# Two-layer convolution and attention encoder on one core: wide gate products, one-product channel mean, reordered first loads, idle products in the last norm

## The chip, the cores and the metric

The kernel runs on one core of a Trainium2 chip. The metric is the time of the device in microseconds, from the start to the end of the program on that core; lower is better. Three runs of the kernel before gave 983.62, 984.91 and 985.09 us, the median is 984.91.

## What is computed

256 positions of width 2048 pass through two layers, all in fp32:

```python
for i in range(2):
    u = _rmsnorm(h, norm_g[i]) @ w_in[i]
    a_val, a_glu, a_z, q, k, v, b_z = split(u)
    ya = silu(_layernorm(conv31(a_val * sigmoid(a_glu)))) * silu(a_z)
    yb = window_attention(q, k, v) * silu(b_z)
    h = h + concatenate([ya, yb]) @ w_out[i]
    e = _rmsnorm(p[i] @ w_pe[i], pe_g[i])
    h = h + e * sigmoid(h @ w_pg[i])
return _rmsnorm(h, final_g)
```

`a_z`, the gate of the convolution group, is what the program calls `za`; `b_z`, the gate of the attention group, is `zb`. `ya` has 1024 channels in 8 tiles of 128, `yb` as well.

## The kernel before

All activations lie channel-first: 128 channels on the partitions, 256 positions along a row. A weight tile is a half of 1024 fp32 columns per partition, that is 8 blocks of 128 x 128. Halves are loaded two at a time, 1 MB, by SP (`load`, L154). Each half is then split into a high part, which ScalarE casts to fp32r (L163), and a low part, which VectorE gets by subtraction (L166). Activations are split in the same way (`hg`, `h`, `ya`, `yb`: index 0 is the high part and index 1 the low part). `mm3` (L387) multiplies a split weight with a split activation. For a 256-column output that is three products, high x high (L394), high x low (L395) and low x high (L396). Where the output is a whole bank of 2 x 256 columns, it is one 512-column product, the weight's high part with both parts of the activation side by side (L391), and one 256-column product (L392); the two sides of the bank must then be added, which `merge` (L398) does with a copy on ScalarE (L402) and an add on VectorE (L403). The output gate `g` uses the wide form (`wide`, L434); the input projection, the convolution gate `za` and the output projection use the narrow one (`pair`, L427).

The order of instructions on TensorE, VectorE and ScalarE is the order in which the program is written (`manual_schedule`, L130). `get` (L184) emits the splits four halves ahead of the products that use them, into five buffers. After each half, `pump` (L198) emits a few convolution taps (VectorE) and one step of every generator in `side`, where the attention heads and the channel norm wait. A bare `yield` in a generator puts what follows off to the next `pump`.

At the end of a layer's gate (L687 to L693) the program emits what is left of the convolutions (`finish`), casts the first pair of `yb` tiles, and applies the gate's Silu. The channel norm `lnorm` (L697) begins at once: the sum over channels is three products with a matrix of ones, of `ysum` (six tiles added up on GpSimd, L565) and of the last two tiles (L702). Its variance goes through `rstd_col` (L338), which multiplies the two halves of `vacc` with a column of ones. The output projection then takes 14 half steps with `yb` (L744), during which the norm finishes `ya`, and 14 with `ya`.

At the start the embedding products `e` (L490) use the first two weight tiles and `p` (L260), while x arrives in four quarters on ScalarE's DMA queue (L272) and ScalarE squares it for the first norm (L377, L380). At the end, `rstd_col` and `rstd_row` make the last norm's factor, three products keep TensorE occupied between them (L845), VectorE multiplies with the factor out of its PSUM bank, and GpSimd with a copy of it that ScalarE makes (L855).

Of the kernel before, what the change touches and what calls it, by code (L numbers as in the profile page):

```python
# [10 lines left out]
F32 = mybir.dt.float32  # L11
# [114 lines left out]
def trunk_kernel(ctx: ExitStack, tc: tile.TileContext, xT, pT, wst, par, gain, relb, sinkp, onehot, out):  # L126
# [136 lines left out]
    def load_half(c, x, n=1):  # L263

        if x == 0:
            raws[c] = wraw.tile([P, 2, HALF], F32, tag="raw", name=f"raw{c}")
        w = HALF // n
        for i in range(n):
            nc.sync.dma_start(raws[c][:, x, i * w:(i + 1) * w], wst[c, :, x * HALF + i * w:x * HALF + (i + 1) * w])

    def load_x(k):
        nc.scalar.dma_start(h[k // 8][:, k % 8:k % 8 + 4, :], xT[:, k:k + 4, :])  # L272

    h = halves(bigt("x"))
    pf = load_p(0)
    load_half(0, 0, 2)

    first = wk.tile([P, 2], F32, name="first", tag="rv")
    nc.scalar.activation(first, zeros[:, 0:2], AF.Square)
    for k in range(0, KT, 4):  # L280
        load_x(k)
    load_half(0, 1)
    load_half(1, 0)
    load_half(1, 1)
    gains = cst.tile([P, (DEPTH + 1) * KT], F32, name="gains")
    nc.sync.dma_start(gains, gain)
    load_half(2, 0)
# [50 lines left out]
    def rstd_col(parts, dim, name, between=None):  # L338

        c = bank(name + "c")  # L340
        for x, a in enumerate(parts):
            for b in range(2):
                nc.tensor.matmul(c[:, 0, b:b + 1], a[:, b * P:(b + 1) * P], ones[:, 0:1],
                                 start=(x == 0 and b == 0), stop=(x == len(parts) - 1), skip_group_check=True)
        v = wk.tile([P, 2], F32, name=name + "v", tag="rv")
        nc.vector.tensor_scalar(v, c[:, 0, 0:2], 1.0 / dim, EPS, ALU.mult, ALU.add)
        col = wk.tile([P, 2], F32, name=name + "col", tag="rcol")
        nc.gpsimd.tensor_tensor(col, v, mhalf, ALU.pow)
        if between:
            between()  # L350
        dg = wk.tile([P, 2, P], F32, name=name + "dg", tag="rdg", bufs=1)
        for b in range(2):
            nc.vector.tensor_scalar(dg[:, b, :], ident, col[:, b:b + 1], None, ALU.mult)
        return dg
# [42 lines left out]

    def merge(bs):  # L398

        t = wk.tile([P, 2, S], F32, name="hl", tag="ptt")[:, 0:len(bs), :]  # L400
        for x, b in enumerate(bs):
            nc.scalar.copy(t[:, x, :], b[:, 1, :])  # L402
            nc.vector.tensor_add(t[:, x, :], b[:, 0, :], t[:, x, :])  # L403
        return t
# [42 lines left out]
    for l in range(DEPTH):  # L447
# [239 lines left out]
        for t in range(0, NCT, 2):  # L687
            b = pair(hg, f"za{l}_{t}")
            if t == NCT - 2:
                finish(l)  # L690
                yb = bigt(f"yb{l}", F32R)
                nc.scalar.copy(yb[:, 0, 0:2, :], zb[:, 0:2, :])
            nc.scalar.activation(za[:, t:t + 2, :], b, AF.Silu)  # L693
# [3 lines left out]
        def lnorm(l=l, acc=acc, za=za, ya=ya, ysum=ysum, done=done):  # L697

            mb = bank("mean")
            parts = [ysum] + [acc[:, t, :] for t in done[-2:]]  # L700
            for x, a in enumerate(parts):
                nc.tensor.matmul(mb[:, 0, :], ones, a, start=(x == 0), stop=(x == len(parts) - 1))  # L702
# [11 lines left out]
            dg = rstd_col(halves_of(vacc), W_CONV, f"rv{l}")  # L714
# [126 lines left out]
    dg = rstd_col(hparts, D, "rf")  # L841

    wb = bank("warm2")
    for _ in range(3):
        nc.tensor.matmul(wb[:, 0, 0:P], ones, ident, start=True, stop=True)  # L845
    rb = rstd_row(dg, "rf", copy=False)
    rbs = wk.tile([P, S], F32, name="rfrb", tag="rb", bufs=1)

    for j in (0, 2, 12, 4, 6, 14, 8, 10):
        for x in [slice(0, 1), slice(1, 2)] if j == 0 else [slice(0, 2)]:  # L850
# [3 lines left out]
            if j == 0 and x.start == 0:  # L854
                nc.scalar.copy(rbs, rb)  # L855
# [78 lines left out]
```

## Time and profile before

| | |
|---|---|
| median of three runs | 984.91 us |
| the profiled execution | 983.99 us |
| its span, first to last instruction | 982.2 us |
| TensorE products, busy share of the span | 98% |
| VectorE | 79% |
| ScalarE | 57% |
| GpSimd | 9% |
| share of TensorE in the chain that ended last | 97% |
| HBM read | 177 MB, 185 GB/s over the span |

The profile comes from one execution. The busy share of an engine counts the time in which at least one of its instructions ran. Products are pipelined: a row's own duration is longer than the distance to the next row, and the distance is what the work costs. The chain that ended last is followed back from the last instruction, at each step to what released it.

### The profile page before, as it was taken

The numbers are of one execution on the slowest core, as the hardware profiler recorded it, in microseconds if no ns is written. First come the engines' busy times: TensorE is split into PE (matmuls) and PEld (weight loads), VectorE is DVE, ScalarE is ACT, GpSimd is POOL, SyncE is SP. The second block draws the span as 40 slices with busy tenths as digits, with TensorE's granted clock in tenths as the row PEclk, the third lists the DMA queues.
The fourth block names the chain that finished last, engine by engine and source line by source line (L and its number), as shares of the span: only waits on it lengthen the run. The fifth ranks groups of instructions, "written<-read, shape, count | busy, mean of one in ns | idle before, by whom it ended". The sixth has DMA issues, their size and how long they took to land.

```text
span 982.2 us, 18152 instructions
## 1 busy us (share of the span) xinstructions
PE 965.8 (98%) x7438; PEld 925.5 (94%) x7438; DVE 774.6 (79%) x1319; ACT 560.0 (57%) x862; POOL 86.6 (9%) x87
## 2 busy tenths in 40 slices
PE   8999999999999999999999999999999999999994
PEld 7999999999999999988899999999999999998884
DVE  4899989987787576687789998988887867667763
ACT  4655454777875554455566444568778545446551
POOL 0022001010000000011103200000100000100111
PEclk9999999999999999999999999999999999999997
DMA  7764636555544466446556555456454445654522
GB/s 287 254 238 171 213 131 215 189 178 181 166 153 177 149 238 225 172 172 230 198 184 237 175 203 181 172 188 204 146 168 165 172 143 200 217 191 162 197 104 86
DMA packets 29135, 182.49 MB, mean 186 GB/s; under 512 B 3723, under 2 KB 4284, under 8 KB 9212
## 3 DMA queue, kind: packets, MB, share of 16 engines
q1 hardware_dynamic: 24284, 165.17, 47.2%
q0 software_dynamic: 3472, 12.88, 4.4%
q10 hardware_dynamic: 1296, 3.28, 0.9%
q8 instruction: 58, 0.95, 0.4%
q14 instruction: 25, 0.20, 0.1%
HBM read 177.09 MB, written 4.23 MB: 185 GB/s over the span
## 4 chain that ended last, share of the span: by engine, by line
PE 97%; DVE 1%; DMA 1%; ACT 0%; POOL 0%; issue 0%; DVEq 0%; SPq 0%; ACTq 0%
PE g L391 12%; PE o L394 6%; PE o L395 6%; PE o L396 6%; PE ag L396 6%; PE ag L394 6%; PE ag L395 6%; PE g L392 6%; PE za L394 3%; PE zb L394 3%; PE q L394 3%; PE q L395 3%; PE zb L395 3%; PE za L395 3%; PE zb L396 3%; PE q L396 3%
## 5 line engine op out<-in xcount | busy, mean ns | idle before, releaser
L166 DVE TENSOR_TENSOR w<-raw,w 128x1024 fp32r<-128x1024 f32 x306 | 372.3, 1227 | 119.1 <-ACT w L163 116.1
L163 ACT CAST w<-raw 128x1024 fp32r<-128x1024 f32 x308 | 316.2, 1047 | 180.2 <-PE ag L396 45.1
L560 DVE SCALAR_TENSOR_TENSOR ac<-ac,pars 128x241 f32<-128x241 f32 (+11 forms) x480 | 217.9, 503 | 1.0
L391 PE MATMUL g<-h,w 128*128 128x512 f32 x496 | 175.3, 399 | 0.0
L396 PE MATMUL ag<-hg,w 128*128 128x256 f32 x512 | 145.2, 284 | 0.5 <-DVE w L166 0.5
L394 PE MATMUL ag<-hg,w 128*128 128x256 f32 x512 | 145.5, 284 | 0.0
L395 PE MATMUL ag<-hg,w 128*128 128x256 f32 x512 | 145.1, 283 | 0.1
L392 PE MATMUL g<-h,w 128*128 128x256 f32 x496 | 139.3, 281 | 0.0
L391 PEld LDWEIGHTS g<-h,w 128*128 128x128 f32 x496 | 93.2, 188 | 23.1
L394 PEld LDWEIGHTS ag<-hg,w 128*128 128x128 f32 x512 | 98.3, 192 | 0.9 <-ACT ac L553 0.9
L396 PEld LDWEIGHTS ag<-hg,w 128*128 128x128 f32 x512 | 98.3, 192 | 0.8 <-DVE w L166 0.7
L395 PEld LDWEIGHTS ag<-hg,w 128*128 128x128 f32 x512 | 98.3, 192 | 0.3 <-DVE hg L467 0.3
L392 PEld LDWEIGHTS g<-h,w 128*128 128x128 f32 x496 | 93.8, 189 | 0.0
L394 PE MATMUL za<-hg,w 128*128 128x256 f32 x256 | 73.7, 288 | 0.0
L394 PE MATMUL o<-yb,w 128*128 128x256 f32 x256 | 73.4, 287 | 0.0
L394 PE MATMUL q<-hg,w 128*128 128x256 f32 x256 | 73.3, 286 | 0.0
L394 PE MATMUL zb<-hg,w 128*128 128x256 f32 x256 | 73.2, 286 | 0.0
L395 PE MATMUL o<-yb,w 128*128 128x256 f32 x256 | 72.6, 284 | 0.0
L396 PE MATMUL o<-ya,w 128*128 128x256 f32 x256 | 72.5, 283 | 0.0
L394 PE MATMUL o<-ya,w 128*128 128x256 f32 x256 | 72.5, 283 | 0.0
L395 PE MATMUL o<-ya,w 128*128 128x256 f32 x256 | 72.5, 283 | 0.0
L396 PE MATMUL o<-yb,w 128*128 128x256 f32 x256 | 72.5, 283 | 0.0
(229 smaller groups left out, 2192.9 us busy)
## 6 DMA issues: line engine op xcount, KB each, us to landing
raw<-in_wst SPq DMA_DIRECT2D x153, 1024.0 KB, 4.9
bias<-fscr POOLq DMA_DIRECT2D x16, 384.0 KB, 3.8
raw<-in_wst SPq DMA_DIRECT2D x5, 512.0 KB, 9.8
x<-in_xT ACTq DMA_DIRECT2D x4, 512.0 KB, 7.1
hx<-in_xT POOLq DMA_DIRECT2D x8, 256.0 KB, 3.6
hscr<-e POOLq DMA_DIRECT2D x2, 1024.0 KB, 4.9
hx<-hscr POOLq DMA_DIRECT2D x8, 256.0 KB, 3.4
out_t<-og ACTq DMA_DIRECT2D x4, 256.0 KB, 3.0
```

What stands on the lines that cost most here:

```text
L163: nc.scalar.copy(hi, raw)
L166: nc.vector.tensor_sub(lo, raw, hi.bitcast(F32))
L391: nc.tensor.matmul(o, w[:, 0], x, start=start, stop=False, skip_group_check=True)
L392: nc.tensor.matmul(o[:, 1], w[:, 1], x[:, 0], start=False, stop=stop, skip_group_check=True)
L394: nc.tensor.matmul(o, w[:, 0], x[:, 0], start=start, stop=False, skip_group_check=True)
L395: nc.tensor.matmul(o, w[:, 0], x[:, 1], start=False, stop=False, skip_group_check=True)
L396: nc.tensor.matmul(o, w[:, 1], x[:, 0], start=False, stop=stop, skip_group_check=True)
L560: nc.vector.scalar_tensor_tensor(acc[:, t, lo_:hi_], a[:, t, lo_ + s:hi_ + s], w(k), acc[:, t, lo_:hi_], ALU.mult, ALU.add)
```

## The change

- `za` uses the wide form: each of the 8 tiles of a layer has a bank of its own and is merged by a copy and an add into its place in `za`; Silu then works on two merged tiles.
- The last two convolution tiles are added to `ysum` on VectorE, and the channel sum is one product. A `yield` ahead of it puts it one half step later.
- The variance's two halves are folded on VectorE ahead of `rstd_col`, which then has two small products instead of four.
- The first loads are dealt out anew over the queues of SP and ScalarE.
- In the last norm, five idle products stand between the small products of the two parts and four behind them; the factor is multiplied out twice, into a bank for VectorE and one for ScalarE's copy.

```diff
-    def load_half(c, x, n=1):
-
-        if x == 0:
+    def load_half(c, x, eng=nc.sync, n=1):
+
+        if c not in raws:
...
-    def load_x(k):
-        nc.scalar.dma_start(h[k // 8][:, k % 8:k % 8 + 4, :], xT[:, k:k + 4, :])
+    def load_x(k, eng=nc.sync):
+        eng.dma_start(h[k // 8][:, k % 8:k % 8 + 4, :], xT[:, k:k + 4, :])
 
     h = halves(bigt("x"))
+
+    load_half(0, 0, nc.scalar, 2)
     pf = load_p(0)
-    load_half(0, 0, 2)
-
-    first = wk.tile([P, 2], F32, name="first", tag="rv")
-    nc.scalar.activation(first, zeros[:, 0:2], AF.Square)
-    for k in range(0, KT, 4):
-        load_x(k)
     load_half(0, 1)
-    load_half(1, 0)
+    load_x(4, nc.scalar)
+    load_x(0)
+    load_half(1, 0, nc.scalar)
+    load_x(8)
+    load_x(12)
     load_half(1, 1)
+    load_half(2, 0)
     gains = cst.tile([P, (DEPTH + 1) * KT], F32, name="gains")
     nc.sync.dma_start(gains, gain)
-    load_half(2, 0)
     load_half(2, 1)
...
+    def idle(n):
+
+        wb = bank("idle")
+        for _ in range(n):
+            nc.tensor.matmul(wb[:, 0, 0:P], ones, ident, start=True, stop=True)
+
+    def rstd_col(parts, dim, name, between=None, idles=0):
 
         c = bank(name + "c")
         for x, a in enumerate(parts):
...
+            if x == 0 and idles:
+                idle(idles)
...
+    def merge1(t, b):
+
+        nc.scalar.copy(t, b[:, 1, :])
+        nc.vector.tensor_add(t, b[:, 0, :], t)
...
         for t in range(0, NCT, 2):
-            b = pair(hg, f"za{l}_{t}")
+            for x in range(2):
+                merge1(za[:, t + x, :], wide(hg, f"za{l}_{t + x}"))
             if t == NCT - 2:
                 finish(l)
+                for d in done[-2:]:
+                    nc.vector.tensor_add(ysum, ysum, acc[:, d, :])
                 yb = bigt(f"yb{l}", F32R)
                 nc.scalar.copy(yb[:, 0, 0:2, :], zb[:, 0:2, :])
-            nc.scalar.activation(za[:, t:t + 2, :], b, AF.Silu)
+            nc.scalar.activation(za[:, t:t + 2, :], za[:, t:t + 2, :], AF.Silu)
...
         def lnorm(l=l, acc=acc, za=za, ya=ya, ysum=ysum, done=done):
 
+            yield
             mb = bank("mean")
-            parts = [ysum] + [acc[:, t, :] for t in done[-2:]]
-            for x, a in enumerate(parts):
-                nc.tensor.matmul(mb[:, 0, :], ones, a, start=(x == 0), stop=(x == len(parts) - 1))
+            nc.tensor.matmul(mb[:, 0, :], ones, ysum, start=True, stop=True)
...
-            dg = rstd_col(halves_of(vacc), W_CONV, f"rv{l}")
+            dg = rstd_col([fold(vacc)], W_CONV, f"rv{l}")
...
-    dg = rstd_col(hparts, D, "rf")
-
-    wb = bank("warm2")
-    for _ in range(3):
-        nc.tensor.matmul(wb[:, 0, 0:P], ones, ident, start=True, stop=True)
+    dg = rstd_col(hparts, D, "rf", idles=5)
+    idle(4)
     rb = rstd_row(dg, "rf", copy=False)
+    rb2 = rstd_row(dg, "rf2", copy=False)
...
-                nc.scalar.copy(rbs, rb)
+                nc.scalar.copy(rbs, rb2)
```

Where it moves instructions, three places matter. The first is the end of the first layer's gate on ScalarE (`z` holds `za` and `zb`, `w` are split weights, `za_6` before is the bank of tiles 6 and 7). Before:

```order
L163 CAST w_3506<-raw_3356 128x1024
L163 CAST w_3534<-raw_3356 128x1024
L692 CAST yb_3561<-z_1613 128x512
L693 ACTIVATE z_1613<-za_6_3434 128x512
L736 CAST yb_3561<-z_1613 128x512 x3
L704 ACTIVATE mu<-mean 128x256
L163 CAST w_3587<-raw_3435 128x1024
```

And of the change:

```order
L163 CAST w_3410<-raw_3287 128x1024
L163 CAST w_3430<-raw_3287 128x1024
L408 COPY z_1611<-za_7_3407 128x256
L707 CAST yb_3453<-z_1611 128x512
L708 ACTIVATE z_1611<-z_1611 128x512
L750 CAST yb_3453<-z_1611 128x512 x3
L163 CAST w_3473<-raw_3352 128x1024
L718 ACTIVATE mu<-mean 128x256
```

The copy of the last gate tile now stands ahead of the first cast of `yb`, and `mu` comes behind one more weight cast.

The second place is the same end on VectorE, up to the variance (`ac` are the convolution tiles). Before:

```order
L166 TENSOR_TENSOR w_3534<-raw_3356,w_3534 128x1024
L737 TENSOR_TENSOR yb_3561<-z_1613,yb_3561 128x512 x4
L166 TENSOR_TENSOR w_3587<-raw_3435,w_3587 128x1024
L709 TENSOR_TENSOR ac_259<-ac_259,mu 128x512 x2
...
L381 TENSOR_TENSOR vacc<-vacc,sq 128x512
L166 TENSOR_TENSOR w_3658<-raw_3504,w_3658 128x1024
L166 TENSOR_TENSOR w_3685<-raw_3504,w_3685 128x1024
L166 TENSOR_TENSOR w_3714<-raw_3585,w_3714 128x1024
L346 TENSOR_SCALAR rv0v<-rv0c 128x2
```

And of the change:

```order
L409 TENSOR_TENSOR z_1611<-za_7_3407,z_1611 128x256
L705 TENSOR_TENSOR ysum_258<-ysum_258,ac_257 128x256 x2
L751 TENSOR_TENSOR yb_3453<-z_1611,yb_3453 128x512 x4
L166 TENSOR_TENSOR w_3473<-raw_3352,w_3473 128x1024
L166 TENSOR_TENSOR w_3504<-raw_3352,w_3504 128x1024
...
L389 TENSOR_TENSOR vacc<-vacc,sq 128x512
L166 TENSOR_TENSOR w_3575<-raw_3408,w_3575 128x1024
L166 TENSOR_TENSOR w_3604<-raw_3471,w_3604 128x1024
L166 TENSOR_TENSOR w_3631<-raw_3471,w_3631 128x1024
L376 TENSOR_TENSOR fold<-vacc 128x256
L354 TENSOR_SCALAR rv0v<-rv0c 128x2
```

Three adds now stand ahead of the low halves of `yb`, and the new fold stands behind three weight splits.

The third place is the start of SP's queue and of ScalarE's (`raw_85`, `raw_93` and `raw_98` are the first three weight tiles in the change). SP, with the change:

```order
L260 DMA p_88<-in_pT 128x512
L269 DMA raw_85<-in_wst 128x1024
L272 DMA x<-in_xT 128x1024 x3
L269 DMA raw_93<-in_wst 128x1024
L269 DMA raw_98<-in_wst 128x1024
```

ScalarE, with the change:

```order
L269 DMA raw_85<-in_wst 128x512 x2
L272 DMA x<-in_xT 128x1024
L269 DMA raw_93<-in_wst 128x1024
L385 ACT_TABLE_LOAD
L385 ACTIVATE hacc<-x 128x512
```

Before, ScalarE's queue held the four quarters of x and SP's `p` and all the weights; now three quarters of x stand on SP and the first half weight tile on ScalarE.

## Rows read from the trace of the kernel before

**Rows 1.** The page, busy time of an engine: us, share of the span, instructions.

```profile
PE 965.8 (98%) x7438; PEld 925.5 (94%) x7438; DVE 774.6 (79%) x1319; ACT 560.0 (57%) x862; POOL 86.6 (9%) x87
```

**Rows 2.** The windows, a stretch in the middle of the first layer's gate: length, then busy us (instructions) of TensorE, its weight loads, VectorE, ScalarE and GpSimd, the granted clock, the DMA share and GB/s.

```profile
250.00:300.00 50.00, 50.00 (x414) 47.35 (x413) 40.65 (x88) 35.12 (x68) 2.02 (x3) 1.00 0.52 172
```

**Rows 3.** The timeline of TensorE: start, duration, line, output and inputs. The first and the last of 24 gate products in a row, then the first and the 23rd 512-column product of the output gate.

```profile
249.84 0.28 PE L394 MATMUL za<-hg,w 128*128 128x256 f32 x1
...
252.60 0.28 PE L396 MATMUL za<-hg,w 128*128 128x256 f32 x1
...
399.99 0.40 PE L391 MATMUL g<-h,w 128*128 128x512 f32 x1
...
407.76 0.40 PE L391 MATMUL g<-h,w 128*128 128x512 f32 x1
```

**Rows 4.** The timeline at the end of the first layer's gate, TensorE, ScalarE and VectorE.

```profile
305.05 0.28 PE L396 MATMUL za<-hg,w 128*128 128x256 f32 x1
...
305.18 0.59 PE L702 MATMUL mean<-ysum,ones 128*128 128x256 f32 x2
...
306.59 0.28 PE L395 MATMUL o<-yb,w 128*128 128x256 f32 x1
...
303.44 0.62 ACT L692 CAST yb<-z 128x512 fp32r<-128x512 f32 x1
...
304.71 0.68 DVE L737 TENSOR_TENSOR yb<-z,yb 128x512 fp32r<-128x512 f32 x1
```

**Rows 5.** The timeline in the second layer's output gate: the product that follows a finished wide tile, the copy and the add of that tile, the VectorE operation behind it, and two adds of which the second needs the first.

```profile
961.04 0.28 PE L394 MATMUL g<-h,w 128*128 128x256 f32 x1
...
961.24 0.37 ACT L402 COPY hl<-g 128x256 f32<-128x256 f32 x1 [1.11 <-PE g L392]
...
961.64 0.42 DVE L403 TENSOR_TENSOR hl<-g,hl 128x256 f32<-128x256 f32 x1 [3.05 <-ACT hl L402]
...
961.99 0.41 DVE L797 TENSOR_TENSOR hs<-h 128x256 f32<-128x256 f32 x1
...
962.61 0.42 DVE L801 TENSOR_TENSOR e<-e,sg 128x256 f32<-128x256 f32 x1 [0.21 <-ACT sg L799]
...
963.07 0.43 DVE L802 TENSOR_TENSOR e<-e,hs 128x256 f32<-128x256 f32 x1
```

**Rows 6.** The timeline of the first channel norm's variance: the four small products (two instructions each) and the second projection product behind them, the row product, the three weight splits on VectorE, and the copy `mu` on ScalarE.

```profile
320.91 0.95 PE L343 MATMUL rv0c<-ones,vacc 128*128 128x1 f32 x8
...
321.92 0.28 PE L395 MATMUL o<-yb,w 128*128 128x256 f32 x1
...
324.68 0.59 PE L359 MATMUL rv0b<-rv0dg,ones 128*128 128x256 f32 x2
...
318.35 3.50 DVE L166 TENSOR_TENSOR w<-raw,w 128x1024 fp32r<-128x1024 f32 x3 [0.25 <-ACT w L163]
...
307.42 0.38 ACT L704 ACTIVATE mu<-mean 128x256 f32<-128x256 f32 x1
```

**Rows 7.** The timeline where the output projection passes from `yb` to `ya`: VectorE's last two low halves of `ya`, and TensorE's last product with `yb`.

```profile
345.86 1.52 DVE L730 TENSOR_TENSOR ya<-ac,ya 128x512 fp32r<-128x512 f32 x2
...
347.91 0.28 PE L395 MATMUL o<-yb,w 128*128 128x256 f32 x1
```

**Rows 8.** The start. First the DMA rate of the first 20 us in 40 equal slices, then two windows (columns as in Rows 2), then rows of the timeline: the first embedding products, the first norm product and a later wait on TensorE; the squares of x and copies on ScalarE; the fold on VectorE.

```profile
GB/s 0 0 0 53 119 397 373 406 299 176 201 205 266 336 344 406 397 414 426 451 393 410 426 418 434 401 410 434 387 390 395 401 393 399 392 426 260 227 475 410
...
8.00:9.00 1.00, 1.00 (x4) 0.77 (x3) 0.49 (x1) 0.48 (x1) 0.00 (x0) 0.50 1.01 406
...
11.00:12.00 1.00, 1.00 (x5) 0.87 (x4) 0.75 (x2) 0.64 (x2) 0.00 (x0) 0.82 1.04 422
...
7.07 10.56 PE L490 MATMUL e<-p,raw 128*128 128x256 f32 x40 [2.25 <-DMA raw<-in_wst]
...
17.46 0.50 PE L343 MATMUL rh0c<-ones,fold 128*128 128x1 f32 x4
...
31.98 0.39 PE L396 MATMUL ag<-hg,w 128*128 128x256 f32 x1 [0.51 <-DVE w L166]
...
7.33 0.63 ACT L377 ACTIVATE hacc<-x 128x512 f32<-128x512 f32 x1 [5.10 <-DMA raw<-in_wst]
...
12.48 0.58 ACT L514 COPY e<-e 128x512 f32<-128x512 f32 x1 [0.84 <-PE e L490]
...
14.21 0.59 ACT L514 COPY e<-e 128x512 f32<-128x512 f32 x1
...
14.69 0.63 ACT L380 ACTIVATE sq<-x 128x512 f32<-128x512 f32 x1
...
16.08 0.42 DVE L368 TENSOR_TENSOR fold<-hacc 128x256 f32<-128x256 f32 x1
```

**Rows 9.** The end: a window (columns as in Rows 2), the last row product on TensorE, VectorE's first and second output multiply, and ScalarE's copy between them.

```profile
971.00:971.50 0.50, 0.32 (x1) 0.35 (x2) 0.03 (x1) 0.00 (x0) 0.00 (x0) 0.50 0.00 0
...
971.18 1.19 PE L359 MATMUL rfb<-rfdg,ones 128*128 128x256 f32 x2 [0.88 <-DVE rfdg L353]
...
972.40 0.42 DVE L853 TENSOR_TENSOR og<-og,rfb 128x256 f32<-128x256 f32 x1 [1.38 <-PE rfb L359]
...
972.86 0.37 ACT L855 COPY rfrb<-rfb 128x256 f32<-128x256 f32 x1 [3.60 <-DVE og L853]
...
973.26 3.41 DVE L853 TENSOR_TENSOR og<-og,rfb 128x256 f32<-128x256 f32 x6 [0.44 <-ACT rfrb L855]
```

More of the change, by code (lines that the diff above doesn't have):

```diff
@@ L268, in load_half @@
         for i in range(n):
-            nc.sync.dma_start(raws[c][:, x, i * w:(i + 1) * w], wst[c, :, x * HALF + i * w:x * HALF + (i + 1) * w])
-    def load_x(k):
-        nc.scalar.dma_start(h[k // 8][:, k % 8:k % 8 + 4, :], xT[:, k:k + 4, :])
+            eng.dma_start(raws[c][:, x, i * w:(i + 1) * w], wst[c, :, x * HALF + i * w:x * HALF + (i + 1) * w])
+    def load_x(k, eng=nc.sync):
+        eng.dma_start(h[k // 8][:, k % 8:k % 8 + 4, :], xT[:, k:k + 4, :])
     h = halves(bigt("x"))
+    load_half(0, 0, nc.scalar, 2)
     pf = load_p(0)
-    load_half(0, 0, 2)
-    first = wk.tile([P, 2], F32, name="first", tag="rv")
-    nc.scalar.activation(first, zeros[:, 0:2], AF.Square)
-    for k in range(0, KT, 4):
-        load_x(k)
-    load_half(0, 1)
-    load_half(1, 0)
+    load_half(0, 1)
+    load_x(4, nc.scalar)
[3 more added lines that the diff above has]
+    load_x(12)
     load_half(1, 1)
+    load_half(2, 0)
     gains = cst.tile([P, (DEPTH + 1) * KT], F32, name="gains")
     nc.sync.dma_start(gains, gain)
-    load_half(2, 0)
     load_half(2, 1)
@@ L335, in load_bias @@
         return t
-    def rstd_col(parts, dim, name, between=None):
+    def idle(n):
[3 more added lines that the diff above has]
+    def rstd_col(parts, dim, name, between=None, idles=0):
         c = bank(name + "c")
@@ L401, in merge @@
         for x, b in enumerate(bs):
-            nc.scalar.copy(t[:, x, :], b[:, 1, :])
-            nc.vector.tensor_add(t[:, x, :], b[:, 0, :], t[:, x, :])
+            merge1(t[:, x, :], b)
         return t
```

## Prediction

> **What bounds the kernel now.** I read the page's busy shares first, then the windows by stage, then the start, the two turns from gate to output projection, and the end. TensorE is busy 98% of the span [rows 1], and in the middle of the convolution gate it is busy for all of 50 us at full clock while VectorE is busy for 40.65 and ScalarE for 35.12 [rows 2]. So time is gained in three ways only: fewer nanoseconds of TensorE per product, shorter TensorE waits at the two ends, or fewer products. And every new TensorE wait is paid in full.
>
> **Gate in 512-column products.** Per weight tile, three 256-column products become one of 512 and one of 256 columns. Old pace: 249.84 to 252.60 us holds 23 steps, 0.1200 each, 0.360 a triple. The output gate runs the new form already: 399.99 to 407.76 is 22 pairs, 0.3532 each [rows 3]. Both layers hold 2 x 8 x 16 = 256 triples, so 256 x 0.0068 = **-1.7 us**. The Trainium skill, page "TensorE: Matmul & The Clock Gate", section "Back-to-back issue gap", spaces warm products by columns / 2.4 GHz plus 2.5 ns; by that estimate triple and pair are 327.5 and 325.0 ns apart and the gain is 0.65 us, and the sum would be 1.1 us higher. The measured pace stands.
>
> The price is a copy on ScalarE and an add on VectorE for each of 16 tiles. Before the last tile of a layer they hide: split weights are made four steps of 2.9 us ahead, and the load rises by 0.37 and 0.42 us in 5.7, from the 70% and 81% of [rows 2].
>
> **The turn to the output projection: a new wait.** In the old program the cast of the first pair of `yb` stood ahead of the last gate instruction on ScalarE and ran at 303.44, its low half on VectorE at 304.71; TensorE's last gate product began at 305.05, so it was through by 305.17 and found both ready [rows 4]. Now the copy of tile 7 stands ahead of that cast, and it waits for TensorE's last gate product; on VectorE the tile-7 add and two `ysum` adds stand ahead of the low half. Call the end of the gate on TensorE T. The output gate shows the same step: TensorE goes on at 961.04, the copy starts at 961.24, the add at 961.64, the next VectorE operation 0.35 later [rows 5]. So: add at T + 0.60, first `ysum` add at T + 0.95, the second, which needs the first, about 0.46 later (the distance of 962.61 to 963.07, two dependent adds, [rows 5]), the first low half at T + 1.76, and with the 0.68 us of [rows 4] it ends at T + 2.45. The cast ends at T + 1.1, so one product runs and the second, which reads the low half, waits until T + 2.5 instead of T + 0.12: 2.4 us, and no other TensorE work stands there, since the change also puts the mean's product one step later. The following low halves are 0.61 apart and are there in time. Two layers: **+4.8 us**. Nothing covers it; neither engine can start before TensorE ends.
>
> **Channel norm.** With three mean products between, the second projection product began at 306.59; two steps of 0.12 after 305.05 would be 305.29 [rows 4]. So they took 1.30 us; one is left, 0.43. Two layers: **-1.7 us**. The variance's four small products took 320.91 to 321.92 less one step, 0.89 us; two are left, -0.45 [rows 6]. But the new fold stands on VectorE behind three weight splits. In the old order those ended at 321.85, 14.4 us after `mu` began at 307.42 [rows 6]. In the new one `mu` begins 3.45 us after the first projection step S (one step of 2.88, the mean, 0.15), the splits end at S + 17.9 and the fold at S + 18.2, while TensorE wants it after six steps and the mean, S + 17.7. It waits 0.5 to 0.6. Both layers: **+0.3 us**. What is late next is `ya`: its last low half ended at 347.38 and TensorE's last `yb` product began at 347.91 [rows 7], with the last pair of `ya` wanted six tiles of 0.36 later; the chain from the variance on moves by the same step as TensorE's, so I cost this at nothing, or 0.5 a layer if that cover is gone.
>
> **First loads.** The first weight piece now leads ScalarE's queue, so the embedding products can follow the warm-up ones instead of starting at 7.07. But x's first quarter now stands third on SP, behind `p` and half a weight tile, and lands together with the second, when `p`, the first weight tile and two quarters of x, 2.36 MB, have come: by the rates in [rows 8], added up, at 9.4 us, where the first square ran at 7.33. ScalarE then needs 1.73 us per group of one copy and two squares (12.48 to 14.21): copies at 10.5, 12.2 and 13.95, last square of the sum at 14.45, against 14.69. The fold, which ended at 16.50, ends near 16.3, and the first norm product can start at once; in the old run TensorE, slowed before, reached it only at 17.46 [rows 8]. What follows it hangs on it, so that distance moves whole: **-1.2 us**. Bounds: 0 if x comes later still, -2.4 if the 400 GB/s of 8 us on were there from 2.5 us, which puts 2.36 MB at 8.2.
>
> **The end.** The final row product took 1.19 us at granted clock 0.50 [rows 9]; the same product took 0.59 at full clock [rows 6] (its work 0.43). Idle products on both sides should hold the clock: -0.75. The second output multiply on VectorE waited for ScalarE's copy of the same bank, 972.40 to 973.26 [rows 9]; with a bank of its own it follows 0.35 later, another -0.45. The second row product costs only GpSimd's side, which still starts earlier. **-1.1 us**; if the clock falls all the same, -0.4.
>
> **TensorE's clock.** The old start shows a wait of 2.25 us ahead of the product at 7.07; 0.9 us after products resumed the granted clock fell to 0.50 and stayed there until 11.4 [rows 8], half of 3.4 us lost, 1.7. The new program has three such waits: 2.4 us at each turn, and about 2.5 us ahead of the first norm product, where the embedding products run out near 13.7. The 0.5 us wait at 31.98 was followed by no fall [rows 8]. Each could cost 0 to 1.7; I take one or two falls, partly beside other waits, **+1.8 us** (bounds 0 and 5.1).
>
> **Sum.** -1.7 + 4.8 - 1.7 + 0.3 - 1.2 - 1.1 + 1.8 = +1.2 us on the profiled execution's 983.99 (span 982.2), which is 0.9 under the median of the three runs, 984.91. So 985.2 for that execution, and **986.1 us** for a median. A measurement of this kernel tells about 0.2% from no change, 2.0 us: this is no change, on the slow side.
>
> **Rivals.**
> - *The clock falls at every new wait* (slower). Price 3 x 1.7 instead of 1.8: 989.4 us. For it: the only wait of that length in the trace did it. Against: the waits are broken by one product, and a fall at the start runs partly beside ScalarE's chain. It decides from the second full fall on. Chance 0.25.
> - *The first loads bring nothing.* The same bytes share the same engines: between 7 and 17 us the DMA runs near 400 GB/s already [rows 8], and x's first quarter comes later. Without the 1.2 us: 987.3. The Trainium skill, "DMA: Bandwidth & Descriptors", section "Issuing engines are not separate DMA queues", says that a second issuing engine saves only the issue time; the trace agrees as far as it goes, but here the order within the queues changes as well. Chance 0.08.
> - *No fall, and the early bytes come at the later rate* (faster). 986.1 - 1.8 - 1.2 = 983.1, and with waits shorter than reckoned below 982.9. For it: the rates of [rows 8] pass 400 GB/s once before 4 us. Chance 0.15.
> - *The idle products don't do what they say*: the clock falls before the last product, the second row product comes at half clock. The end gains 0.4: 986.8. Chance 0.07.
> - The forecast as summed: 0.45.
>
> **Numbers.** Faster 0.15; within 0.2% the forecast and the last rival, 0.52; slower the first two, 0.33. The range is 982.8 to 989.6: down to the third rival, up to the first.
>
> **What would show it.** Right: TensorE idle 2 to 2.5 us per layer ahead of the first two products `o<-yb`, put down to ScalarE's `yb` and VectorE's `yb`; gate pairs 0.353 apart; a first square near 9.4 and the first norm product near 16.3; `rfb` in about 0.45 us. Wrong: no idle time at the turns (then the result is 4 to 5 us faster), gate products waiting for banks or weights, or a first square before 8.

## The result, and the profile after

The changed kernel takes **987.21 us** (median of 18 executions, 984.60 to 988.71); the kernel before, run beside it, 984.14 us. The ratio is 1.0027, 95% interval 1.0020 to 1.0033: slower by a little more than the 0.2% that can be told. It lies inside the range of the prediction, above its 986.1 us and on the slow side, where "slower by over 0.2%" had 0.33; the outcome that the prediction held likeliest, within 0.2%, did not come. Two single executions among the experiments below, at 1891 and 2417 us, were in a slow state and are left out of every time given.

The profiled execution of the changed kernel is the quickest of the 18, 984.60 us with a span of 982.8. A fall below means that TensorE's granted clock goes from 1.00 to 0.50, that is from 2.4 to 1.2 GHz; in this execution there is none before the output multiplies. The others stand in steps above it: seven at 985.45 to 985.89, six at 987.09 to 987.88, four at 988.40 to 988.71, with a mean granted clock that goes down from 0.997 to 0.992. What the trace shows is therefore the change without falls of the clock; what a fall costs is read further down, from two traces that have two each.

**The page, and the gate's stretch** (compare [rows 1] and [rows 2]; columns as there).

```profile
PE 965.0 (98%) x7180; PEld 911.1 (93%) x7180; DVE 781.3 (79%) x1341; ACT 564.3 (57%) x877; POOL 86.7 (9%) x87
...
250.00:300.00 50.00, 50.00 (x306) 41.77 (x305) 41.50 (x92) 37.02 (x72) 2.02 (x3) 1.00 0.49 167
```

TensorE is as full as before, with 258 product instructions fewer in all. VectorE has 0.85 us more in these 50 us, ScalarE 1.9, and both have room left.

**The gate's pace** (timeline of TensorE; compare [rows 3]). The first and the eighth 512-column product of the gate:

```profile
249.18 0.40 PE L399 MATMUL za<-hg,w 128*128 128x512 f32 x1
...
251.65 0.40 PE L399 MATMUL za<-hg,w 128*128 128x512 f32 x1
```

Seven pairs in 2.47 us are 0.353 each, the pace that the output gate had.

**The turn to the output projection** (timeline of TensorE, then ScalarE, then VectorE; compare [rows 4]).

```profile
303.41 0.28 PE L400 MATMUL za<-hg,w 128*128 128x256 f32 x1
304.67 0.38 PE L402 MATMUL o<-yb,w 128*128 128x256 f32 x1 [0.98 <-ACT yb L707]
306.11 0.39 PE L403 MATMUL o<-yb,w 128*128 128x256 f32 x1 [1.05 <-DVE yb L751]
306.33 0.28 PE L404 MATMUL o<-yb,w 128*128 128x256 f32 x1
...
308.96 0.59 PE L716 MATMUL mean<-ysum,ones 128*128 128x256 f32 x2
...
303.72 0.37 ACT L408 COPY z<-za 128x256 f32<-128x256 f32 x1 [1.72 <-PE za L400]
303.99 0.62 ACT L707 CAST yb<-z 128x512 fp32r<-128x512 f32 x1
...
309.60 0.38 ACT L718 ACTIVATE mu<-mean 128x256 f32<-128x256 f32 x1 [1.77 <-PE mean L716]
...
303.10 1.22 DVE L166 TENSOR_TENSOR w<-raw,w 128x1024 fp32r<-128x1024 f32 x1
304.24 0.42 DVE L409 TENSOR_TENSOR z<-za,z 128x256 f32<-128x256 f32 x1
304.57 0.87 DVE L705 TENSOR_TENSOR ysum<-ysum,ac 128x256 f32<-128x256 f32 x2
305.37 0.68 DVE L751 TENSOR_TENSOR yb<-z,yb 128x512 fp32r<-128x512 f32 x1
```

The gate ends at T = 303.53, 0.12 after its last product begins. The first product with `yb` runs at T + 1.14, the second at T + 2.58. Between them stand exactly the instructions named: copy and cast on ScalarE; tile 7's add, the two `ysum` adds and the low half on VectorE. VectorE was still busy with a weight split when the copy was done, so tile 7's add began at T + 0.71. Layer 2 has the same waits, 0.98 and 1.05.

**The variance** (TensorE, then VectorE; compare [rows 6]).

```profile
324.63 0.58 PE L349 MATMUL rv0c<-ones,fold 128*128 128x1 f32 x4 [0.68 <-DVE fold L376]
...
320.65 3.50 DVE L166 TENSOR_TENSOR w<-raw,w 128x1024 fp32r<-128x1024 f32 x3 [0.25 <-ACT w L163]
324.07 0.42 DVE L376 TENSOR_TENSOR fold<-vacc 128x256 f32<-128x256 f32 x1
```

**The start** (TensorE, ScalarE, VectorE; compare [rows 8]).

```profile
16.80 0.50 PE L349 MATMUL rh0c<-ones,fold 128*128 128x1 f32 x4
...
9.69 0.63 ACT L385 ACTIVATE hacc<-x 128x512 f32<-128x512 f32 x1 [5.73 <-DMA x<-in_xT]
...
15.79 0.42 DVE L376 TENSOR_TENSOR fold<-hacc 128x256 f32<-128x256 f32 x1
```

**The end** (TensorE, VectorE, ScalarE; compare [rows 9]).

```profile
972.75 0.67 PE L367 MATMUL rfb<-rfdg,ones 128*128 128x256 f32 x2 [0.65 <-DVE rfdg L361]
...
973.45 3.74 DVE L865 TENSOR_TENSOR og<-og,rfb 128x256 f32<-128x256 f32 x7 [0.85 <-PE rfb L367]
...
973.88 0.37 ACT L867 COPY rfrb<-rf2b 128x256 f32<-128x256 f32 x1 [3.05 <-PE rf2b L367]
```

The row product takes 0.67 instead of 1.19, and VectorE multiplies seven times without a break.

Where TensorE stands in the two traces, in us, by the start of the product named:

| | before | changed | difference |
|---|---|---|---|
| first projection product | 24.27 | 23.62 | -0.65 |
| first gate product, layer 1 | 249.84 | 249.18 | -0.66 |
| last gate product, layer 1 | 305.05 | 303.41 | -1.64 |
| first product with `ya`, layer 1 | 348.15 | 348.61 | +0.46 |
| first gate product, layer 2 | 726.09 | 726.54 | +0.45 |
| last gate product, layer 2 | 781.30 | 780.77 | -0.53 |
| first product with `ya`, layer 2 | 824.40 | 825.97 | +1.57 |
| `rfb` | 971.18 | 972.75 | +1.57 |
| end of the span | 982.2 | 982.8 | +0.6 |

The gate gives 0.98 a layer, the turn with the norm takes 2.10 back, the start gives 0.65 and the end 0.97.

### The profile page after: what moved, and what is told of

Its sections match the earlier page's. It is cut to its first block, busy times and chain, and to the rows that moved or that the text cites. A ratio compares the mean times of both kernels' runs of the same rounds, so it can differ in the third digit from the quotient of the medians.

```text
span 982.8 us, 17671 instructions
## 1 busy us (share of the span) xinstructions
PE 965.0 (98%) x7180; PEld 911.1 (93%) x7180; DVE 781.3 (79%) x1341; ACT 564.3 (57%) x877; POOL 86.7 (9%) x87
## 4 chain that ended last, share of the span: by engine, by line
PE 87%; DVE 7%; ACT 3%; issue 1%; DMA 0%; POOL 0%; DVEq 0%; ACTq 0%
PE g L399 12%; PE ag L404 6%; PE ag L402 6%; PE ag L403 6%; PE g L400 6%; PE o L403 5%; PE o L404 5%; PE o L402 5%; PE zb L402 3%; PE q L402 3%; PE zb L403 3%; PE q L403 3%; PE zb L404 3%; PE q L404 3%; DVE w L166 3%; PE za L399 3%
## 5 line engine op out<-in xcount | busy, mean ns | idle before, releaser
L399 PE MATMUL za<-hg,w 128*128 128x512 f32 x256 | 92.2, 402 | 0.0
```

Of the source, the lines that this page charges most:

```text
L399: nc.tensor.matmul(o, w[:, 0], x, start=start, stop=False, skip_group_check=True)
```

## Experiments

My theory was the prediction's: the loss is TensorE's wait at the two turns, and in the other executions a fall of its clock there. The rivals: the spread comes from the new start; the wide tiles alone make the wait; something else is late next. Times are medians, with the lowest and the highest execution behind them.

**Order at the turn (e_turn).** A gate tile takes two half steps, one for each weight half; in tile 7 all of `yb` now goes between them, and GpSimd adds the last two convolution tiles to `ysum`:

```diff
-            if 2 <= len(done) <= NCT - 2:
+            if 2 <= len(done):
...
-                merge1(za[:, t + x, :], wide(hg, f"za{l}_{t + x}"))
+                b = bank(f"za{l}_{t + x}")
+                step(b, hg, True, False)
+                if t + x == NCT - 1:
...
+                    for i in range(0, 8, 2):
+                        hilo(yb[:, 0, i:i + 2, :], yb[:, 1, i:i + 2, :], zb[:, i:i + 2, :])
+                step(b, hg, False, True)
+                merge1(za[:, t + x, :], b)
...
-                for d in done[-2:]:
-                    nc.vector.tensor_add(ysum, ysum, acc[:, d, :])
```

> The change, but all four casts and low halves of yb are put between the two half steps of gate tile 7, and the last two convolution tiles are added to ysum on GpSimd; the rest is as changed. Theory A (the loss is TensorE's wait at the two turns, 0.98 + 1.05 us per layer in the profiled execution, and in other executions a fall of the clock at these waits): no wait at the turn, 2 x 2.0 = 4.1 us gone, and with it the 2.6 us by which the median of 18 runs, 987.21, stands above the execution without a fall, 984.6: about 980.6 us, single runs within some 1 us. Rival B (the spread of single runs comes from the start or from elsewhere): 987.2 - 4.1 = 983.1 us, and single runs still 4 us apart. Rival C (the wait is hidden by something else that is late next, such as ya): 985 to 987 us with a new wait ahead of the ya products.

985.06 us (983.12 to 987.56). The wait at the turn shrank as meant, but the theory's 980.6 us failed: rival C came true, at the variance instead of `ya`. Waits of TensorE in this trace (what it waited for: us in total, times, longest):

```profile
PE rv1c L349 <- DVE fold L376: 1.9, 1, 1.9
...
PE rv0c L349 <- DVE fold L376: 1.0, 1, 1.0
PE o L403 <- DVE yb L456: 1.0, 3, 0.4
...
PE mean L721 <- POOL ysum L577: 0.5, 1, 0.5
```

ScalarE's timeline of layer 2 shows why; the mean began at 783.75:

```profile
784.28 0.63 ACT L713 ACTIVATE z<-z 128x512 f32<-128x512 f32 x1 [3.70 <-DVE z L409]
784.81 1.03 ACT L163 CAST w<-raw 128x1024 fp32r<-128x1024 f32 x1
785.75 0.38 ACT L723 ACTIVATE mu<-mean 128x256 f32<-128x256 f32 x1
```

`mu` stands behind Silu, which waits for VectorE's add of tile 7, and behind a weight cast: 2.0 us after the mean, where the change has 0.64. Counted from the first gate product of layer 2, TensorE's second `yb` product had become 1.9 us earlier than in the change, `mu` only 0.1: the norm's chain kept its old time. After the 1.9 us wait the clock fell to 0.50, at 801.

**Idle products in the turn (e_idle).**

```diff
  ob = [bank(f"o{l}_{j}") for j in range(NB_FIRST // 2)]
+ idle(9)
```

> The change plus nine idle products between the last gate product and the first product of the output projection in each layer, some 2.4 us of TensorE work that nothing needs: the turn is as long, but TensorE is occupied in it. Theory A (the clock falls at the turns in other executions than the profiled one): 984.6 to 985.2 us, single runs within some 1.5 us. Rival B (falls or spread from elsewhere): 987.2 us, single runs 4 us apart as before.

984.90 us (984.10 to 986.47): 2.3 us less than the change, with work added. The turn is as long, the second `yb` product at T + 2.59, and the trace has no fall there; so what went is the clock's falls at the turns. Some spread is left. In the profiled execution TensorE waited 1.3 us for the first norm's fold and the clock fell at 18, which puts at least a part of it at the start.

**Narrow gate (e_narrow).**

```diff
- for x in range(2):
-     merge1(za[:, t + x, :], wide(hg, f"za{l}_{t + x}"))
+ b = pair(hg, f"za{l}_{t}")
...
- nc.scalar.activation(za[:, t:t + 2, :], za[:, t:t + 2, :], AF.Silu)
+ nc.scalar.activation(za[:, t:t + 2, :], b, AF.Silu)
```

> The change with the convolution gate narrow again (a bank of two tiles, three 256-column products, Silu out of the bank); ysum on VectorE, one mean product, loads and end as changed. The gate takes 1.7 us more. Theory A (add and ysum adds both stand in the way; without the add the two ysum adds and the low half still come 1.2 to 1.4 us after the gate's end, because VectorE is through with its weight splits only then): 984.6 + 1.7 - 2 x 0.7 = 984.9 us without falls, 985 to 987 as a median. Rival D (the copy and the add of the wide tile alone make the wait): 984.6 + 1.7 - 4.1 = 982.2 us, with a narrow spread.

983.88 us (983.47 to 985.24), between the two, and 3.3 us below the change:

```profile
PE o L403 <- DVE yb L750: 1.6, 2, 0.8
```

TensorE waits 0.8 us per layer, before the second product alone, because the `ysum` adds (303.75 to 304.55) still stand ahead of the low half. So the wide tile makes about 1.2 of the 2.0 us. With waits of 0.8 us the executions lie within 1.8 us, and the trace has no fall at either turn. The other four parts of the change together are worth nothing that can be told against the kernel before: ratio 1.0001 (0.9992 to 1.0009).

**Old first loads (e_loads).**

```diff
-    load_half(0, 0, nc.scalar, 2)
     pf = load_p(0)
+    load_half(0, 0, n=2)
...
+    for k in range(0, KT, 4):
+        load_x(k, nc.scalar)
     load_half(0, 1)
-    load_x(4, nc.scalar)
-    load_x(0)
-    load_half(1, 0, nc.scalar)
-    load_x(8)
-    load_x(12)
+    load_half(1, 0)
     load_half(1, 1)
-    load_half(2, 0)
...
```

> The change with the first loads in the old order on the old queues. Theory A: the first gate-side product comes 0.65 us later, as in the two traces (24.27 against 23.62), and the spread at the turns stays: 987.2 + 0.7 = 987.9 us. Rival B (the new start is what makes single runs differ by 4 us): a narrow spread, about 985.3 us. Rival E (the reordered loads bring nothing): 987.2 us.

986.61 us, which eight executions do not tell from the change's 987.21; theory A's 987.9 failed. The eight lie on three levels: 985.10 and 985.22; 986.53, 986.58 and 986.63; 988.21, 988.21 and 988.51. Steps of 1.4 and 1.7 us would fit none, one or two falls at the turns, but only the execution at 985.22 has a trace (it has none), and the one at 986.53 has a mean granted clock of 0.997, the same as that trace, in which 3.4 us at half clock, 0.0017 of the mean, do not fit. With 3.4 us of spread left, the new start is not what makes the change's 4.1. That it adds to it is seen across the traces: with the new loads the first projection product comes anywhere from 23.04 to 24.86 (the nine traces that start as the change does), with the old from 24.02 to 24.32 (four).

**Reordered version (e_best).** Against the change:

```diff
-            if 2 <= len(done) <= NCT - 2:
+            if 2 <= len(done) <= NCT - 1:
...
+                step(b, hg, True, False)
+                if t + x == NCT - 1:
...
+                    for i in range(0, 8, 2):
+                        hilo(yb[:, 0, i:i + 2, :], yb[:, 1, i:i + 2, :], zb[:, i:i + 2, :])
+                        if i == 2:
+                            nc.vector.tensor_add(ysum, ysum, acc[:, done[-1], :])
+                step(b, hg, False, True)
...
             nc.scalar.mul(mu, mb[:, 0, :], 1.0 / W_CONV)
+            nc.scalar.activation(za[:, NCT - 2:NCT, :], za[:, NCT - 2:NCT, :], AF.Silu)
...
+            fv = fold(vacc)
             yield from wait(LY[0])
-            dg = rstd_col([fold(vacc)], W_CONV, f"rv{l}")
+            dg = rstd_col([fv], W_CONV, f"rv{l}")
```

> The change with three orders of work altered and nothing else: the casts and low halves of yb stand between the two half steps of gate tile 7, with the add of the last convolution tile to ysum between them (the tile before it is added on GpSimd); the last Silu of za stands behind the cast mu; the fold of vacc stands ahead of the three weight splits. Theory F (in the first such run the gain was eaten by VectorE's and ScalarE's queue: mu came 2.0 us after the mean instead of 0.64, because Silu and a weight cast stood ahead of it, and the fold then kept TensorE 1.0 and 1.9 us): both waits go, 2 x (2.03 - 0.5) + 2 x 0.7 = 4.5 us less than the execution without falls, 980.1 us; median 980 to 981.5 us, the rest being the start. Rival G (the two layer ends are bound by VectorE's total work from the gate to ya, so that a wait comes back ahead of the last ya products or of the variance): 983 to 985 us.

**979.63 us** (978.64 to 980.08, five executions), ratio to before 0.9949 (0.9936 to 0.9961): 4.4 us below the kernel before. Theory F holds. Of the turn, 0.4 us per layer are left, of the variance nothing; the one fall in its trace is at the start.

```profile
PE rh0c L349 <- DVE fold L376: 1.3, 1, 1.3
...
PE o L403 <- DVE yb L456: 0.8, 2, 0.4
```

**Old mean (e_mean).**

```diff
-                for d in done[-2:]:
-                    nc.vector.tensor_add(ysum, ysum, acc[:, d, :])
...
-            yield
             mb = bank("mean")
-            nc.tensor.matmul(mb[:, 0, :], ones, ysum, start=True, stop=True)
+            parts = [ysum] + [acc[:, t, :] for t in done[-2:]]
+            for x, a in enumerate(parts):
+                nc.tensor.matmul(mb[:, 0, :], ones, a, start=(x == 0), stop=(x == len(parts) - 1))
```

> The change with the old mean: three products at once behind the gate, ysum of six tiles alone, no half step's delay; wide gate, fold, loads and end as changed. Theory A (at the turn the copy, the add and the ysum adds all stand ahead of yb, and the mean's products no longer cover it): the three products cover 1.3 us, the low half of yb ends 0.87 us earlier, 0.3 us of 2.03 remain; minus 2 x 1.7, plus 2 x 0.87 for the products: 984.6 - 1.7 = 982.9 us without falls, and as the waits are short, no falls: median 983 to 983.8 us. Rival D (the wide tile's copy and add alone make the wait): 984.6 + 1.7 = 986.3 us or more.

985.07 us (983.91 to 986.38), five of the eleven executions at 983.91 to 984.49; theory A's 983 to 983.8 was missed.

```profile
PE rv0c L349 <- DVE fold L376: 1.3, 1, 1.3
...
PE o L403 <- DVE yb L750: 1.1, 4, 0.3
```

The turn behaved as meant (two waits of up to 0.3 per layer, no falls there in the trace), so rival D is out; but the fold now keeps TensorE 1.3 us per layer instead of 0.7. With the mean one half step earlier, the variance's products come earlier too, and the three splits ahead of the fold do not.

**Fold ahead of the splits (e_fold).**
```diff
+ fv = fold(vacc)
  yield from wait(LY[0])
- dg = rstd_col([fold(vacc)], W_CONV, f"rv{l}")
+ dg = rstd_col([fv], W_CONV, f"rv{l}")
```

> The change with the fold of vacc ahead of the three weight splits on VectorE. Theory: TensorE's 0.7 us wait ahead of the variance goes in both layers, 1.4 us less: 983.2 us without falls, median 985.5 to 986 us, the turns being as they are. Rival G (ya is late next: its last low half ended 0.05 us before TensorE wanted it): the gain is lost again ahead of the last ya products, 987 us.

985.64 us (984.65 to 986.79). The wait ahead of the variance is gone, and none came ahead of `ya`: as expected. The profiled execution happens to have the clock's fall at both turns. Windows of layer 1 (columns as in [rows 2], the granted clock is the third number from the end):

```profile
304.50:305.00 0.50, 0.00 (x0) 0.00 (x0) 0.50 (x2) 0.50 (x2) 0.00 (x0) 1.00 1.00 164
305.00:305.50 0.50, 0.00 (x0) 0.00 (x0) 0.50 (x2) 0.50 (x2) 0.00 (x0) 1.00 0.44 82
305.50:306.00 0.50, 0.47 (x4) 0.48 (x5) 0.50 (x2) 0.50 (x2) 0.00 (x0) 1.00 0.86 279
306.00:306.50 0.50, 0.50 (x7) 0.50 (x6) 0.50 (x2) 0.50 (x2) 0.00 (x0) 1.00 0.85 360
306.50:307.00 0.50, 0.50 (x6) 0.50 (x5) 0.50 (x2) 0.50 (x1) 0.00 (x0) 0.71 1.08 459
307.00:308.00 1.00, 1.00 (x7) 1.00 (x7) 1.00 (x2) 0.24 (x1) 0.00 (x0) 0.50 0.89 377
308.00:309.00 1.00, 1.00 (x6) 1.00 (x6) 0.50 (x1) 0.00 (x0) 0.00 (x0) 0.50 0.01 0
309.00:309.50 0.50, 0.50 (x5) 0.50 (x4) 0.00 (x0) 0.00 (x0) 0.00 (x0) 0.50 0.00 0
309.50:310.00 0.50, 0.50 (x3) 0.50 (x3) 0.00 (x0) 0.00 (x0) 0.00 (x0) 0.50 0.00 0
310.00:310.50 0.50, 0.50 (x4) 0.38 (x4) 0.00 (x0) 0.00 (x0) 0.00 (x0) 0.88 0.00 0
```

The waits end at 305.52; about a microsecond after TensorE has resumed, its clock is at 1.2 GHz, until just after 310. Measured by the mean's product, which comes at 309.67 where a start 0.57 earlier than the change's should put it at 308.39, the first fall had cost 1.3 us by then, with 0.45 us of the half clock still to come. The second one, measured in the same way, costs 1.4.

**The wide gate alone, in the kernel before (e_bwide).**

```diff
- b = pair(hg, f"za{l}_{t}")
+ for x in range(2):
+     b = wide(hg, f"za{l}_{t + x}")
+     nc.scalar.copy(za[:, t + x, :], b[:, 1, :])
+     nc.vector.tensor_add(za[:, t + x, :], b[:, 0, :], za[:, t + x, :])
...
- nc.scalar.activation(za[:, t:t + 2, :], b, AF.Silu)
+ nc.scalar.activation(za[:, t:t + 2, :], za[:, t:t + 2, :], AF.Silu)
```

> The kernel before with the wide convolution gate alone (copy and add per tile, Silu on merged tiles); mean, variance, loads and end as before. Theory A: gate -1.7; the turn covered by the three mean products up to 0.3 to 0.5 us, + 2 x 0.4: 984.1 - 0.9 = 983.2 us. Rival D (copy and add alone make a wait of 2 us per layer): 984.1 - 1.7 + 4 = 986.4 us. Rival H (the wide gate needs more VectorE and ScalarE than there is in the gate window): 984.1 us or more, with waits ahead of za products.

983.98 us (983.66 to 985.16), ratio 0.9995 (0.9986 to 1.0004): no change. The mean's products begin 1.25 us earlier than in the old trace and the variance's 0.23, with the start 0.26 earlier: what the gate gained, 0.99 in layer 1, is given back whole inside the turn. The old three mean products do cover most of the new wait, but VectorE and ScalarE, one copy and one add behind, then deliver each of the first two low halves late:

```profile
303.82 0.28 PE L392 MATMUL za<-hg,w 128*128 128x256 f32 x1
...
305.07 0.43 PE L394 MATMUL o<-yb,w 128*128 128x256 f32 x1
305.80 0.39 PE L395 MATMUL o<-yb,w 128*128 128x256 f32 x1 [0.29 <-DVE yb L740]
...
306.50 0.28 PE L394 MATMUL o<-yb,w 128*128 128x256 f32 x1
307.02 0.39 PE L395 MATMUL o<-yb,w 128*128 128x256 f32 x1 [0.24 <-DVE yb L740]
```

A wait that the trace puts at 0.29 costs 0.6: the products stand 0.73 apart instead of 0.12. The idle column alone understates it.

**Old end (e_tail).**

```diff
-    dg = rstd_col(hparts, D, "rf", idles=5)
-    idle(4)
+    dg = rstd_col(hparts, D, "rf")
+    idle(3)
     rb = rstd_row(dg, "rf", copy=False)
-    rb2 = rstd_row(dg, "rf2", copy=False)
...
-                nc.scalar.copy(rbs, rb2)
+                nc.scalar.copy(rbs, rb)
```

> The change with the old last norm: three products between, one row product that VectorE and ScalarE's copy share, no idle products between the two parts of the sum. Theory: the end gives 1.0 us in the two traces (from the last row product on, 0.97), so 985.6 us without falls at the turns, and 1.0 us above the change's 987.2 us as a median: 988.2 us. Rival (the end's gain is only the profiled execution's): 987.2 us.

986.79 us (985.01 to 988.05), below what theory and rival both expected; the lowest two executions 985.01 and 985.12, 0.45 above the change's quickest. With the spread of both programs the median cannot tell 1.0 from nothing. In its trace the clock held until the row product was through, which took 0.67 at full clock; from `rfb` to the span's end it is 10.5 us, against 10.1 with the change and 11.0 before. By these three traces the second bank gives about 0.45, and the idle products give their 0.5 only in executions in which the clock would have fallen; no run has the two apart.

This trace shows something else as well. Up to the last norm its program is the change's, it has the same waits at both turns, and after both the clock fell: 0.50 in the two windows below (columns as in [rows 2]). The last two rows are the first product with `ya` of layer 2, in this trace and in the change's:

```profile
308.00:309.00 1.00, 1.00 (x7) 1.00 (x7) 1.00 (x1) 0.00 (x0) 0.00 (x0) 0.50 0.49 205
787.00:788.00 1.00, 1.00 (x6) 1.00 (x6) 0.97 (x1) 0.00 (x0) 0.00 (x0) 0.50 0.36 148
...
829.02 0.28 PE L402 MATMUL o<-ya,w 128*128 128x256 f32 x1
...
825.97 0.28 PE L402 MATMUL o<-ya,w 128*128 128x256 f32 x1
```

It comes 3.05 us later with the two falls, of which 0.04 was there before the first gate: 1.5 us for each fall.

**Reordered, with the narrow gate (e_best_narrow).** Against the reordered version:

```diff
+            b = bank(f"za{l}_{t}")
...
-                b = bank(f"za{l}_{t + x}")
-                step(b, hg, True, False)
+                step(b[:, x, :], hg, x == 0, False)
...
-                step(b, hg, False, True)
-                merge1(za[:, t + x, :], b)
+                step(b[:, x, :], hg, False, True)
...
-                nc.scalar.activation(za[:, t:t + 2, :], za[:, t:t + 2, :], AF.Silu)
+                nc.scalar.activation(za[:, t:t + 2, :], b, AF.Silu)
...
-            nc.scalar.activation(za[:, NCT - 2:NCT, :], za[:, NCT - 2:NCT, :], AF.Silu)
+            nc.scalar.activation(za[:, NCT - 2:NCT, :], zlast, AF.Silu)
```

> The reordered version (yb between the half steps of the last gate tile, Silu behind mu, fold ahead of the splits) with the gate narrow again. Theory (once nothing waits at the turn, the wide gate is worth its pace): + 2 x 0.85, 981.3 us. Rival H (the wide tiles' copies and adds still cost something at the turn): 980 us or less.

979.34 us (979.21 to 980.82), not to be told from 979.63. Rival H holds: in the two traces the wide gate gains 0.98 us a layer over the narrow one up to the last gate product and has lost 0.75 of it when the mean begins, where the low halves of `yb` come 0.4 us late because VectorE has add, split and a last tap in hand. With the narrow gate it is idle 0.85 us before them.

**Reordered, with the old loads (e_best_loads).** The edit of the old first loads on top of the reordered version.

> The reordered version with the first loads in the old order. Theory (the new order brings the first projection product 0.6 us forward, but where the embedding products then end early, TensorE waits 1.3 us for the first norm's sum and its clock falls in part of the executions, 1.6 us, so that the median has nothing of it): 979.3 to 979.9 us with little spread, the same as the 979.63 us of the version with the new loads. Rival (the new order brings 0.6 us in the median): 980.3 us.

980.03 us (979.92 to 981.08), 0.4 above, with overlapping ranges and between theory and rival: nothing that can be told.

**Reordered, with the first norm's parts in another order (e_best_swap).**

```diff
- hparts = [fold(hacc)] + halves_of(sq)
+ hparts = halves_of(sq) + [fold(hacc)]
```

> The reordered version in which the first norm's sum takes the last two x tiles' squares first and the folded sum last, so that only two small products, 0.4 us instead of 1.4, stand behind the fold. Theory: TensorE waits 0.65 us less and VectorE's factor comes 0.65 us earlier, and falls of the clock there are rarer: 978.0 us without a fall, median 978 to 979 us. Rival (the first norm is bound by the operands behind it, on VectorE and ScalarE): 979.6 us.

978.62 us (978.05 to 979.80), the best of all, ratio to before 0.9947 (0.9935 to 0.9960). It is 1.0 below the other reordered version, as the theory had it; five executions of each do not separate that safely. Nor is the mechanism shown: in this trace TensorE was late with the embedding products and had no wait ahead of the first norm product to lose, and the version with the narrow gate, whose profiled execution was as late, has none there in the old order of the parts. What goes with TensorE's being late or early there stands in the last section.

## Why the prediction was right, and which term was off

- **Gate pace: right.** -1.7 forecast, -1.96 in the trace. The estimate from the Trainium skill's page "TensorE: Matmul & The Clock Gate", section "Back-to-back issue gap", 0.65, is too small here. What I had not seen: almost none of the gain stays. Alone in the old kernel the wide gate is worth 0.
- **The turn: right in mechanism, place and size.** T + 2.5 forecast for the second product, T + 2.58 measured, waits put down to the two instructions named.
- **Turn and norm together: 0.4 us a layer too low.** The forecast's net for both layers is +4.8 - 1.7 + 0.3 = +3.4, the trace has +4.2. TensorE waits 0.68 for the fold instead of 0.5 to 0.6, and behind each of three waits the next products stand up to 0.1 wider apart (306.11 to 306.33). The `ya` cover held in every run.
- **First loads: a value that only some executions have.** -1.2 forecast, -0.65 in this execution; two other traces with the same loads (the old mean, the early fold) have the first projection product at 23.04 and 23.05, which is -1.2, and in two (the idle products, the reordered version) it comes at 24.86 and 24.68, later than the old 24.27. Of the reason, the first square at 9.7 for 9.4 and the fold near 16.2 were right. The step that failed is "the first norm product can start at once": in the change's trace TensorE was at half clock until 10.6 and reached that product at 16.80, and in the four traces in which it was early it waited 1.3 us for the fold. In the median of the kernel the new loads do not show (986.61 and 980.03 us without them, 987.21 and 979.63 with them). The Trainium skill's page "DMA: Bandwidth & Descriptors", section "Issuing engines are not separate DMA queues", lets a second issuing engine save only issue time. The first embedding product came from 7.07 to 5.61 here, but no run separates the second engine from the new order.
- **The end: right in the profiled execution.** -1.1 forecast, -0.97 measured. Its two parts, -0.75 and -0.45, add up to -1.2 and not to -1.1, and the first of them is there only where the clock would have fallen.
- **The clock: the mis-sized term.** +1.8 forecast, as one or two falls partly beside other waits. The median of the 18 stands 2.6 above the execution without one. A fall costs 1.3 to 1.5 us, near the 1.7 that I had read off the old start. Idle products in the turns take 2.3 us of it away, which shows where most falls come from. Two falls at 1.5 us put an execution at 984.6 + 3.0 = 987.6, in the middle of the group at 987.09 to 987.88. The highest, at 988.40 to 988.71, have something more; a fall at the start as in the two traces just named, in which the first projection product comes 1.1 to 1.2 later than in the change's, would make 988.7 to 988.8, the first rival's case. Which falls each of the 18 had no trace shows.
- **The base: luck.** The forecast added its terms to a median of three runs, 984.91; that of 18 is 984.14, so 0.8 of the closeness of 986.1 to 987.21 is owed to a base that was too high. The change itself is +3.1 us, against +1.2 forecast. By the trace the terms are -1.96 (gate) + 4.2 (turns and norms) - 0.65 (start) - 0.97 (end), and 2.6 for the clock: +3.2.

Without falls the change would still not be faster. The spans of the two traces are 982.8 and 982.2 us, the quickest executions 984.60 and 982.98, and with idle products in the turns the ratio to the kernel before is 1.0008 (1.0000 to 1.0017). Most of what makes it slower is the clock, and most of the clock's falls belong to the two turns.

## What to carry to other kernels

When TensorE is the bound, a faster product is worth only what the engines that feed the next stage can follow: look at the first instruction behind the stage's end on every engine, not at the stage. Products that look like waste, the old three for the mean, can be the cover of a hand-over; before they are removed, the operands behind them have to be moved ahead of the end. And a wait of two microseconds on TensorE is priced with the half clock that may follow it, which one profile can miss: read the single executions beside the profile.

## What the runs showed of the hardware

- The same wait is followed by a fall of the clock in one execution and not in the next: 0.98 + 1.05 us at both turns, no fall in the trace of the change, two in those of the early fold and of the old end, at almost the same times.
- The windows print a granted clock of 1.00 at the start, where TensorE can be at half pace. Two windows of the change, then one of the early fold:

```profile
8.00:9.00 1.00, 1.00 (x4) 0.82 (x3) 0.00 (x0) 0.00 (x0) 0.00 (x0) 1.00 1.04 426
12.00:13.00 1.00, 1.00 (x7) 0.87 (x6) 0.90 (x2) 1.00 (x3) 0.00 (x0) 1.00 1.02 406
...
8.00:9.00 1.00, 1.00 (x6) 0.90 (x5) 0.00 (x0) 0.00 (x0) 0.00 (x0) 1.00 1.05 426
```

  In the change the embedding products' instructions stand 0.427 us apart up to 10.46 and 0.216 from 10.76 on; in the early fold they are 0.216 apart from 6.37 on, but for one step. The trace's record of the granted clock has its first entry, 1.00, at 10.62 and at 6.33, just where the pace doubles, and none before: the 1.00 of an earlier window is no measurement. The start goes with this first rise. Of the ten traces with the new loads, the four in which it comes at 4.3 to 6.4 have a wait of 1.3 us for the first norm's sum, and in the two of these where it comes at 4.3 and 4.4 the clock fell at 18; the six in which it comes at 9.3 to 10.6 have no such wait, and no fall at the start.
- In the second layer of the first reordering GpSimd's add ran beside VectorE's four low halves of `yb`: one of them took 1.22 us, the others 0.68 (3.02 for the four from 779.75, against 2.49 from 305.37 in the change). In its first layer VectorE's four kept their time and GpSimd's add took 3.95 us, against 1.02 in the second (spans on GpSimd are rough in this profile); TensorE then waited 0.5 us for it ahead of the mean.
